# Second input projection: convolutions accumulated in PSUM, transposes behind the next product

## The chip, the cores and the metric

The kernel runs on one NeuronCore of a Trainium2 chip. The metric is the device time of one execution in microseconds. The engines are called as in the profile: PE is TensorE (PEld its weight loads), DVE VectorE, ACT ScalarE, POOL GpSimd, SP the queue that issues most DMAs. PSUM has eight banks of 512 fp32 columns on 128 partitions; a tile of 128x1024 fp32 takes two of them.

## The reference

Two transformer-like blocks over 1024 tokens of width 1024 in fp32. The first (gated recurrence and attention, then a mixture of 16 experts) isn't touched. Of the second, the change touches what follows:

```python
h = layer_norm(x, ln_emb_g, ln_emb_b)
proj = jnp.einsum('bld,de->ble', h, w_in[i])
xs, z, bm, cm, dt_raw, glu, cgate = jnp.split(proj, SPLITS_2, axis=-1)
xbc = jax.nn.silu(causal_depthwise_conv(concatenate([xs, bm, cm]), ssm_conv_w, ssm_conv_b))   # 4 taps
dt = jax.nn.softplus(dt_raw + dt_bias);  a = -jnp.exp(a_log)
y = ssd_chunked(xh, dt, a, bm_c, cm_c) + d_skip * xh      # 8 chunks of 128 tokens, decays exp(cumsum)
yz = y * silu(z)                                          # then a normalisation in 2 groups
u = (glu[..., :1024] + b) * sigmoid(glu[..., 1024:] + b)
u = causal_depthwise_conv(u, conf_conv_w, conf_conv_b)    # 31 taps
u = silu(layer_norm(u)) * silu(cgate)
```

## The kernel before

Products are taken in three matmuls each (`mm3`, L136): every fp32 operand is split into a high part, a cast by ACT, and a low part, a subtraction by DVE or POOL (`split`, L127). A product of a 128-channel tile with 1024 tokens is 48 matmuls of 512 columns into a two-bank PSUM tile "big", of which there are three (pool `pq`, L1213); one more two-bank tile "tr" (pool `pt1`, L1214) takes transposes.

`in_proj2` (L1198) normalises the input in two halves (`turned`, L1219: transposes, the high part by ACT, a full-precision copy `hf` in SBUF, the low part by DVE or POOL), then calls, in an order written out at L1426 to L1442, for j = 0 to 7 `glu(j)`, and between them `bc` (B and C), `dts` (step sizes) and `xs` (four calls), and then the gate products `z`.

`glu(j)` makes two products and `u`, and `conv_tail` (L1270) its 31-tap convolution: tap 0 and taps 1 to 5 as scaled passes by ACT, added up on POOL into `acc` in SBUF, and taps 6 to 30 as `scalar_tensor_tensor` on DVE. The DVE taps go into a list `bgq` with a cost each, from which `bg(us)` (L1092) emits as many as its budget allows, after each product. `last` stores `acc` and adds it to `s1` on POOL.

`xbc` (L1324) copies a product into SBUF (`xl`, ACT), convolves it with four DVE instructions, applies Silu on ACT, and, for B and xs, transposes the result on PE straight away into "tr"; `bc` and `xs` copy that out. `dts` does the same for the step sizes, then a `log1p` chain of small DVE instructions and two matmuls of prefix sums. `s1`, when all eight convolutions are added, is summed over channels on PE (`chan_sum`, L1449) in the middle of `z(2)`, and `mu` in SBUF is subtracted in `centred`.

The state-space part (`decays` L1605, `chunk` L1633, `ssd` L1695) makes for each chunk the decay matrix `M`: DVE and POOL scale triangles, PE sums them into a one-bank tile "seg" (two of them), ACT writes the exponential into SBUF, and DVE multiplies it by `cbm`. `chunk` uses the PSUM tiles "po" (twice) and "pyd".

The program is written with a framework that orders each engine's instructions when it is built, by an estimate of its own of when each can start (L1897), and puts in the semaphores; on the chip each engine runs its list in that fixed order and waits where an operand or a buffer isn't ready. So instructions that stand together in the code, as the four of a convolution, may stand apart with taps between them.

Of the kernel before, what the change touches and what calls it, by code (L numbers as in the profile page):

```python
# [18 lines left out]
P = 128  # L19
S = 1024  # L20
# [17 lines left out]
NPT = 6  # L38
# [74 lines left out]
class Core:  # L113
# [1084 lines left out]
    def in_proj2(self, cl):  # L1198
# [20 lines left out]
        def turned(half, xts):  # L1219

            hs = slice(half * 512, half * 512 + 512)
            for k2 in range(KT // 2):
                pt = pq.tile([P, 2, 512], F, name="big") if half == 0 and k2 % 3 else pt1.tile([P, 2, 512], F, name="tr")
                hf = st.tile([P, S + 4], F, name="xl")[:, 0:D].rearrange("p (a b) -> p a b", a=2)
                for q in range(2):
# [44 lines left out]
        def conv_tail(j, u):  # L1270
            acc = cf.tile([P, S], F, name="acc", bufs=3)
            w = lambda t: self.col("conf_conv_w", j * 31 + t)
            nc.scalar.activation(acc, u[:, 0:S], AF.Identity, bias=self.col("conf_conv_b", j), scale=w(0))
            for t in range(1, NPT):
                tmp = cf.tile([P, S], F, name="tmp")
                nc.scalar.activation(tmp, u[:, t:t + S], AF.Copy, scale=w(t))  # L1276
                nc.gpsimd.tensor_add(acc, acc, tmp)  # L1277

            def tap(t):
                nc.vector.scalar_tensor_tensor(acc, u[:, t:t + S], w(t), acc, op0=ALU.mult, op1=ALU.add)  # L1280

            def last():
                nc.sync.dma_start(self.ucd[j * P:(j + 1) * P, :], acc)
                if j == 0:
                    nc.gpsimd.tensor_copy(s1, acc)
                else:
                    nc.gpsimd.tensor_add(s1, s1, acc)
# [8 lines left out]
        def glu(j):  # L1296
# [25 lines left out]
            self.bg(17.0)  # L1322

        def xbc(j, ps, dst):  # L1324

            xl = st.tile([P, S + 4], F, name="xl")
            nc.vector.memset(xl[:, 0:3], 0.0)
            nc.scalar.copy(xl[:, 3:S + 3], ps)
            a = ct(0)
            w = lambda t: self.col("ssm_conv_w", j * 4 + t)  # L1330
            nc.vector.tensor_scalar(a, xl[:, 0:S], w(0), self.col("ssm_conv_b", j), op0=ALU.mult, op1=ALU.add)
            for t in range(1, 4):
                nc.vector.scalar_tensor_tensor(a, xl[:, t:t + S], w(t), a, op0=ALU.mult, op1=ALU.add)
            nc.scalar.activation(dst, a, AF.Silu)
            pt = pt1.tile([P, NB, P], F, name="tr")
            if j < 10:
                for b in range(NB):
                    nc.tensor.transpose(pt[:, b], dst[:, b * P:(b + 1) * P], self.ident)
            return pt

        def bc(which):
            w = weights(W[:, 2048 + which * 256:2304 + which * 256])
            dst = (self.BT, self.CT)[which]
            for g in range(2):
                pt = xbc(8 + which * 2 + g, proj(w, g), dst[:, g])
                if which == 0:
                    nc.scalar.copy(self.Bk[:, :, g * P:(g + 1) * P], pt)
                self.bg(5.0)

        def xs(jj):  # L1350
            w = weights(W[:, jj * 256:(jj + 1) * 256])
            for i in range(2):
                j = jj * 2 + i
                t = ct(1)
                pt = xbc(j, proj(w, i), t)
                o = st.tile([P, NB, P], F, name="t2", bufs=1)
                nc.scalar.copy(o, pt)
                nc.sync.dma_start(self.xsd[:, j * P:(j + 1) * P].rearrange("(b p) c -> p b c", p=P), o)
                self.bg(5.0)

        def dts():
# [3 lines left out]
            raw = st.tile([NE, S], F, name="t2", bufs=1)  # L1365
# [4 lines left out]
            cut = Cut(ct(1))  # L1370
# [11 lines left out]
            adt = cut.tile([P, P], F, "adt").rearrange("p (b h) -> p b h", b=NB)  # L1382
            nc.vector.scalar_tensor_tensor(adt, self.dt, -1.0, al[:, None, :].to_broadcast([P, NB, NE]), op0=ALU.mult,
                                           op1=ALU.mult)
            self.split(self.adtH, self.adtL, adt)
            self.adtH, self.adtL = self.adtH.bitcast(F), self.adtL.bitcast(F)
            pt = pt1.tile([P, NB, P], F, name="tr")
            nc.tensor.matmul(pt[:, 0], self.U, f(adt), start=True, stop=True)
            nc.tensor.matmul(pt[:, 1], self.ones, f(adt), start=True, stop=True)
            tot = cut.tile([P, P], F, "tot")  # L1390
            nc.scalar.copy(tot, pt[:, 1])
            nc.vector.tensor_sub(e, tot, pt[:, 0])
            nc.scalar.activation(e, e, AF.Exp)
            nc.vector.tensor_mul(f(self.ddt), f(self.dt), e)
            nc.scalar.activation(f(self.cdec), tot, AF.Exp)
            nc.scalar.activation(f(self.eacs), pt[:, 0], AF.Exp)
# [52 lines left out]
        def chan_sum(s):  # L1449
            ps = pq.tile([P, S], F, name="big")  # L1450
# [450 lines left out]
```

## Time and profile before

| | us |
|---|---|
| median of 3 runs (lowest, highest) | 2415.98 (2408.94, 2416.17) |
| the profiled execution | 2410.97 |
| its span, first to last instruction | 2409.0 |
| PE busy | 2103.6 |
| DVE busy | 2006.4 |
| ACT busy | 1151.8 |
| POOL busy | 742.4 |
| mean granted clock of TensorE | 0.932 |

The span is the time from the first to the last instruction of the profiled execution. A group's line gives the total busy time, the mean of one instruction and the idle time of the engine just before them, with what ended it. The list of waits says who waited for whom. The granted clock is 1.0 where the engine runs at 2.4 GHz and 0.5 where it runs at 1.2; a mean between them is a mix of the two.

### The profile page before, as it was taken

Reading aid. Unit: us, or ns where it says so; the run is one execution under the profiler, and the core shown is the slowest. Engines: PE = TensorE matmul, PEld = TensorE weight load, DVE = VectorE, ACT = ScalarE, POOL = GpSimd, SP = SyncE. Lnnn points to the kernel's source line nnn. Section 1 sums busy time; section 2 is a strip of 40 time slices with the busy share of each in tenths; the row PEclk is TensorE's granted clock in tenths of the full one; section 3 lists DMA queues with packets and bytes.
Section 4 is the critical chain, followed back from the end, with each engine's and each line's share of the span. In section 5 each row is a group of like instructions: output and inputs, shape, how many; then the busy total and the mean of one; then the engine's idle time right before and its main releaser. Section 6 shows DMA issues by size and latency. Waiting matters only on the chain. (4 is left out here: it accounts for less than half of the span.)

```text
span 2409.0 us, 26895 instructions
## 1 busy us (share of the span) xinstructions
PE 2103.6 (87%) x10158; PEld 1725.8 (72%) x10158; DVE 2006.4 (83%) x2389; ACT 1151.8 (48%) x1365; POOL 742.4 (31%) x320
## 2 busy tenths in 40 slices
PE   4899899979899999988996978677796988788997
PEld 3678679868778888777884766556595876567785
DVE  8687869977878998878897399999998779995776
ACT  4484749842257777656775433232222443334111
POOL 2333300030202122112211455444552266563000
PEclk8899999989889999999997989888898998889999
DMA  7433373137489999988984111122224453336212
GB/s 251 149 126 116 117 175 99 65 95 283 151 335 369 386 379 393 358 295 309 393 307 132 45 27 53 35 70 61 61 71 150 156 202 122 122 114 244 76 56 70
DMA packets 213857, 422.88 MB, mean 176 GB/s; under 512 B 46144, under 2 KB 118080, under 8 KB 213600
## 3 DMA queue, kind: packets, MB, share of 16 engines
q1 hardware_dynamic: 198528, 380.27, 45.5%
q0 software_dynamic: 9440, 34.61, 4.7%
q10 hardware_dynamic: 5760, 6.29, 0.7%
q8 instruction: 80, 1.31, 0.2%
q14 instruction: 49, 0.40, 0.0%
HBM read 362.35 MB, written 58.77 MB: 175 GB/s over the span
## 5 line engine op out<-in xcount | busy, mean ns | idle before, releaser
L130 ACT CAST wH<-wr 128x2048 fp32r<-128x2048 f32 (+1 forms) x262 | 437.8, 1678 | 206.4 <-PE big L143 156.3
L134 DVE TENSOR_TENSOR wL<-wr,wH 128x2048 fp32r<-128x2048 f32 (+1 forms) x197 | 463.2, 2369 | 82.6 <-ACT wH L130 81.2
L1280 DVE SCALAR_TENSOR_TENSOR acc<-u,cols,acc 128x1024 f32<-128x1024 f32 x200 | 364.9, 1856 | 1.9
L141 PE MATMUL big<-hL,wH 128*128 128x512 f32 (+1 forms) x720 | 289.3, 403 | 6.3 <-DVE hL L326 6.2
L140 PE MATMUL big<-hH,wH 128*128 128x512 f32 (+1 forms) x720 | 284.1, 400 | 9.4 <-ACT B L410 3.7
L134 POOL TENSOR_TENSOR wL<-wr,wH 128x1024 fp32r<-128x1024 f32 (+2 forms) x66 | 188.8, 2871 | 251.2 <-ACT wH L130 236.1
L143 PE MATMUL big<-hH,wL 128*128 128x512 f32 (+1 forms) x720 | 232.4, 401 | 0.0
L140 PEld LDWEIGHTS big<-hH,wH 128*128 128x128 f32 (+1 forms) x720 | 137.5, 191 | 43.5 <-ACT hH L324 4.4
L141 PEld LDWEIGHTS big<-hL,wH 128*128 128x128 f32 (+1 forms) x720 | 138.5, 192 | 39.5 <-DVE hL L326 6.5
L143 PEld LDWEIGHTS big<-hH,wL 128*128 128x128 f32 (+1 forms) x720 | 138.0, 192 | 31.5 <-issue 0.9
L140 PE MATMUL big<-hH,aH 128*128 128x512 f32 x384 | 154.3, 403 | 6.3 <-ACT aH L130 2.8
L140 PE MATMUL big<-wH,0H 128*128 128x512 f32 x384 | 152.6, 397 | 3.6 <-ACT 0H L130 3.6
L141 PE MATMUL big<-wL,1H 128*128 128x512 f32 x384 | 153.7, 400 | 2.3 <-DVE wL L134 2.3
L141 PE MATMUL big<-wL,0H 128*128 128x512 f32 x384 | 154.1, 401 | 0.0
L141 PE MATMUL big<-hL,aH 128*128 128x512 f32 x384 | 152.9, 399 | 0.9 <-DVE hL L1526 0.9
L140 PE MATMUL big<-wH,1H 128*128 128x512 f32 x384 | 151.5, 395 | 2.0 <-ACT 1H L130 2.0
L140 PE MATMUL big<-wH,hH 128*128 128x256 f32 (+1 forms) x448 | 151.3, 338 | 1.9 <-ACT B L410 1.7
L141 PE MATMUL big<-wL,hH 128*128 128x256 f32 (+1 forms) x448 | 149.1, 333 | 0.0
L143 PE MATMUL big<-wH,hL 128*128 128x256 f32 (+1 forms) x448 | 148.8, 332 | 0.0
L1005 POOL DMA_INDIRECT xe<-h2d,idx x16 | 43.4, 2710 | 339.9 <-issue 252.3
L1277 POOL TENSOR_TENSOR acc<-acc,tmp 128x1024 f32<-128x1024 f32 x40 | 124.5, 3114 | 34.5 <-ACT tmp L1276 18.5
L143 PE MATMUL big<-wH,1L 128*128 128x512 f32 x384 | 120.4, 395 | 7.6 <-DVE 1L L134 7.6
(539 smaller groups left out, 4842.0 us busy)
## 6 DMA issues: line engine op xcount, KB each, us to landing
wr<-in_w_dram SPq DMA_DIRECT2D x192, 1024.0 KB, 8.3
wr<-in_w_in_dram SPq DMA_DIRECT2D x48, 512.0 KB, 6.5
wm<-in_w_mod_dram SPq DMA_DIRECT2D x32, 512.0 KB, 4.0
wm<-in_w_mod_dram SPq DMA_DIRECT2D x8, 1024.0 KB
wr<-in_w_in_dram SPq DMA_DIRECT2D x32, 256.0 KB, 3.1
u<-ucd SPq DMA_DIRECT2D x16, 512.0 KB, 3.4
wr<-in_w_out_dram SPq DMA_DIRECT2D x14, 512.0 KB, 6.1
xt<-in_x_dram SPq DMA_DIRECT2D x12, 512.0 KB, 9.1
```

The costliest lines, as they stand in the source:

```text
L130: self.high = nc.scalar.copy(h, src)
L134: (le or nc.vector).tensor_sub(l, src, h)
L140: mm(o, aH, bH, start=start, stop=False)
L141: mm(o, aH, bL, start=False, stop=False)
L143: mm(o, aL, bH, start=False, stop=stop)
L1005: nc.gpsimd.indirect_dma_start(out=xe, out_offset=None, in_=self.h2d, in_offset=bass.IndirectOffsetOnAxis(ap=idx[:, :1], axis=0))
L1277: nc.gpsimd.tensor_add(acc, acc, tmp)
L1280: nc.vector.scalar_tensor_tensor(acc, u[:, t:t + S], w(t), acc, op0=ALU.mult, op1=ALU.add)
```

## The change

`conv_tail` accumulates in the PSUM tile "tr": ACT writes tap 10 with the bias (`begin`), DVE adds taps 11 to 30 there, ACT and POOL make a side sum `part` of taps 0 to 9 in SBUF, its steps put between the taps, and DVE joins both in `last`. `xbc` reads the product from PSUM. The transposes, the step sizes (`steps`) and the prefix sums (`sums`) go into a list `later` that `proj` runs after its own matmuls, into "big" tiles. `turned` keeps the scaled copy in PSUM. `mu` lies in "tr". In the state space, the exponential stays in "seg", and the tiles "po"/"pyd" become "y" (for the outputs of both kinds) and "s" (for the states). `bg` budgets and costs change. "..." marks what is left out.

```diff
-NPT = 6
+NPT = 10
...
-                hf = st.tile([P, S + 4], F, name="xl")[:, 0:D].rearrange("p (a b) -> p a b", a=2)
...
                     if half:
-                        nc.vector.tensor_scalar(hf[:, q], pt[:, q], g, b, op0=ALU.mult, op1=ALU.add)
+                        nc.vector.tensor_scalar(pt[:, q], pt[:, q], g, b, op0=ALU.mult, op1=ALU.add)
                     else:
-                        self.evac = nc.scalar.activation(hf[:, q], pt[:, q], AF.Identity, bias=b, scale=g)
-                    (nc.gpsimd if q else nc.vector).tensor_sub(hL[k][:, hs], hf[:, q], hH[k][:, hs])
+                        self.evac = nc.scalar.activation(pt[:, q], pt[:, q], AF.Identity, bias=b, scale=g)
+                    nc.vector.tensor_sub(hL[k][:, hs], pt[:, q], hH[k][:, hs])
...
+        later = []
+
+        def after():
+            fns = later[:]
+            later.clear()
+            for fn in fns:
+                fn()
...
                          kt == 0, kt == KT - 1)
+            after()
             return ps
...
         def conv_tail(j, u):
-            acc = cf.tile([P, S], F, name="acc", bufs=3)
+
             w = lambda t: self.col("conf_conv_w", j * 31 + t)
-            nc.scalar.activation(acc, u[:, 0:S], AF.Identity, bias=self.col("conf_conv_b", j), scale=w(0))
-            for t in range(1, NPT):
-                tmp = cf.tile([P, S], F, name="tmp")
-                nc.scalar.activation(tmp, u[:, t:t + S], AF.Copy, scale=w(t))
-                nc.gpsimd.tensor_add(acc, acc, tmp)
+            acc, part = [], []
+
+            def begin():
+                acc.append(pt1.tile([P, S], F, name="tr"))
+                nc.scalar.activation(acc[0], u[:, NPT:NPT + S], AF.Identity, bias=self.col("conf_conv_b", j), scale=w(NPT))
+
+            def side(t):
+                if t == 0:
+                    part.append(cf.tile([P, S], F, name="acc", bufs=3))
+                    nc.scalar.activation(part[0], u[:, 0:S], AF.Copy, scale=w(0))
+                else:
+                    tmp = cf.tile([P, S], F, name="tmp")
+                    nc.scalar.activation(tmp, u[:, t:t + S], AF.Copy, scale=w(t))
+                    nc.gpsimd.tensor_add(part[0], part[0], tmp)
 
             def tap(t):
-                nc.vector.scalar_tensor_tensor(acc, u[:, t:t + S], w(t), acc, op0=ALU.mult, op1=ALU.add)
+                nc.vector.scalar_tensor_tensor(acc[0], u[:, t:t + S], w(t), acc[0], op0=ALU.mult, op1=ALU.add)
 
             def last():
-                nc.sync.dma_start(self.ucd[j * P:(j + 1) * P, :], acc)
+                nc.vector.tensor_add(part[0], acc[0], part[0])
+                nc.sync.dma_start(self.ucd[j * P:(j + 1) * P, :], part[0])
...
-            for t in range(NPT, 31):
-                self.bgq.append((1.13, lambda t=t: tap(t)))
-            self.bgq.append((0.0, last))
+            side(0)
+            self.bgq.append((0.0, begin))
+            for i, t in enumerate(range(NPT + 1, 31)):
+                if i % 2 == 0 and i // 2 + 1 < NPT:
+                    self.bgq.append((0.0, lambda t=i // 2 + 1: side(t)))
+                self.bgq.append((1.22, lambda t=t: tap(t)))
+            self.bgq.append((1.22, last))
...
-            self.bg(17.0)
+            self.bg(15.0)
 
         def xbc(j, ps, dst):
 
-            xl = st.tile([P, S + 4], F, name="xl")
-            nc.vector.memset(xl[:, 0:3], 0.0)
-            nc.scalar.copy(xl[:, 3:S + 3], ps)
             a = ct(0)
             w = lambda t: self.col("ssm_conv_w", j * 4 + t)
-            nc.vector.tensor_scalar(a, xl[:, 0:S], w(0), self.col("ssm_conv_b", j), op0=ALU.mult, op1=ALU.add)
-            for t in range(1, 4):
-                nc.vector.scalar_tensor_tensor(a, xl[:, t:t + S], w(t), a, op0=ALU.mult, op1=ALU.add)
+            nc.scalar.activation(a, ps, AF.Identity, bias=self.col("ssm_conv_b", j), scale=w(3))
+            for k in range(1, 4):
+                nc.vector.scalar_tensor_tensor(a[:, k:S], ps[:, 0:S - k], w(3 - k), a[:, k:S], op0=ALU.mult, op1=ALU.add)
             nc.scalar.activation(dst, a, AF.Silu)
-            pt = pt1.tile([P, NB, P], F, name="tr")
-            if j < 10:
-                for b in range(NB):
-                    nc.tensor.transpose(pt[:, b], dst[:, b * P:(b + 1) * P], self.ident)
-            return pt
+
+        def turn(src, fn):
+
+            pt = pq.tile([P, NB, P], F, name="big")
+            for b in range(NB):
+                nc.tensor.transpose(pt[:, b], src[:, b * P:(b + 1) * P], self.ident)
+            fn(pt)
...
-                pt = xbc(8 + which * 2 + g, proj(w, g), dst[:, g])
+                xbc(8 + which * 2 + g, proj(w, g), dst[:, g])
                 if which == 0:
-                    nc.scalar.copy(self.Bk[:, :, g * P:(g + 1) * P], pt)
-                self.bg(5.0)
+                    later.append(lambda g=g: turn(dst[:, g], lambda pt: nc.scalar.copy(self.Bk[:, :, g * P:(g + 1) * P], pt)))
+                self.bg(7.0)
...
-                pt = xbc(j, proj(w, i), t)
-                o = st.tile([P, NB, P], F, name="t2", bufs=1)
-                nc.scalar.copy(o, pt)
-                nc.sync.dma_start(self.xsd[:, j * P:(j + 1) * P].rearrange("(b p) c -> p b c", p=P), o)
-                self.bg(5.0)
+                xbc(j, proj(w, i), t)
+                later.append(lambda j=j, t=t: turn(t, lambda pt: store(j, pt)))
+                self.bg(7.0)
...
-            pt = pt1.tile([P, NB, P], F, name="tr")
+            later.append(lambda: steps(raw))
+
+        def steps(raw):
+
+            pt = pq.tile([P, NB, P], F, name="big")
...
+            def sums():
+                pt = pq.tile([P, NB, P], F, name="big")
+                nc.tensor.matmul(pt[:, 0], self.U, adt, start=True, stop=True)
...
+            later.append(sums)
...
-        mu = cp.tile([P, S], F, name="mu")
-        z(2, mid={ZM: [lambda: nc.scalar.activation(mu, chan_sum(s1), AF.Copy, scale=1.0 / D)]})
+        mu = pt1.tile([P, S], F, name="tr")
+        z(2, mid={ZM: [lambda: nc.scalar.activation(mu, chan_sum(s1, mu), AF.Copy, scale=1.0 / D)]})
...
-                    M = Mg[:, q * 4:q * 4 + 4]
-                    nc.scalar.activation(M.rearrange("p h l -> p (h l)"), sg, AF.Exp)
-                    nc.vector.tensor_mul(M, M, cbm[:, None, :].to_broadcast([P, 4, P]))
+                    nc.scalar.activation(sg, sg, AF.Exp)
+                    nc.vector.tensor_mul(Mg[:, q * 4:q * 4 + 4], sg.rearrange("p (h l) -> p h l", l=P),
+                                         cbm[:, None, :].to_broadcast([P, 4, P]))
...
-                po = psum("po")
+                po = psum("y")
...
-                ps = psum("po")
+                ps = psum("s")
...
-            pyd = psum("pyd")
+            pyd = psum("y")
...
-            nc.vector.tensor_add(xs, pyd, xs)
-            nc.vector.tensor_mul(xs, xs, sz)
+            nc.vector.tensor_add(pyd, pyd, xs)
+            nc.vector.tensor_mul(xs, pyd, sz)
```

## Rows read from the trace of the kernel before

**Rows 1.** The page's slices of the whole span, busy tenths in 40 slices

```profile
DVE  8687869977878998878897399999998779995776
...
PEclk8899999989889999999997989888898998889999
```

**Rows 2.** Table of stretches: us of each engine busy (instructions), clock, DMA

```profile
1372.60:1845.00 472.40, 362.65 (x1823) 304.67 (x1823) 460.57 (x301) 145.84 (x152) 244.14 (x80) 0.88 0.19 57
1845.00:1945.00 100.00, 100.00 (x455) 81.95 (x456) 68.48 (x44) 38.45 (x37) 26.39 (x15) 0.98 0.50 169
1990.00:2150.00 160.00, 132.34 (x567) 102.08 (x566) 154.22 (x168) 57.66 (x147) 99.10 (x48) 0.87 0.33 112
```

**Rows 3.** List of waits, PE alone, 1372.6 to 1866: total us, times, longest

```profile
PE tr L1338 <- ACT t L1334: 47.5, 3, 17.1
PE tr L1388 <- DVE t L1383: 21.1, 1, 21.1
PE big L1452 <- POOL s L1287: 20.1, 1, 20.1
PE tr L1338 <- ACT BT L1334: 12.1, 2, 11.0
PE tr L1369 <- ACT t L1366: 8.7, 1, 8.7
```

**Rows 4.** Table of stretches again, after one wait and in a stretch without

```profile
1480.00:1500.00 20.00, 18.99 (x77) 15.65 (x78) 20.00 (x18) 7.51 (x10) 9.56 (x3) 0.82 0.16 53
1640.00:1660.00 20.00, 20.00 (x89) 16.33 (x87) 19.82 (x12) 8.63 (x8) 16.00 (x6) 1.00 0.18 53
```

**Rows 5.** Groups of instructions, DVE, 1372.6 to 1845: busy us, mean ns, idle before

```profile
L1280 DVE SCALAR_TENSOR_TENSOR acc<-u,cols,acc 128x1024 f32<-128x1024 f32 x200 | 364.9, 1856 | 1.9
L1333 DVE SCALAR_TENSOR_TENSOR t<-xl,cols,t 128x1024 f32<-128x1024 f32 x36 | 56.1, 1557 | 0.1
L1320 DVE SCALAR_TENSOR_TENSOR u<-t,t 128x1024 f32<-128x1024 f32 x8 | 14.5, 1816 | 4.6 <-ACT t L1317 4.1 <-ACT t L1315 0.5
```

**Rows 6.** POOL: one line's shortest/median/longest ns, then a group of 1372.6 to 1845

```profile
L1277 POOL TENSOR_TENSOR acc<-acc,tmp x40: 2393/3260/3566, 1377.8 to 1786.6; 128x1024 f32<-128x1024 f32 x40
...
L134 POOL TENSOR_TENSOR wL<-wr,wH 128x1024 fp32r<-128x1024 f32 x30 | 93.1, 3109 | 91.4 <-ACT wH L130 88.2 <-PE big L141 3.2
```

**Rows 7.** Timelines of DVE and POOL, 1396 to 1440: start us, us, instruction, count

```profile
1399.45 13.32 DVE L1280 SCALAR_TENSOR_TENSOR acc<-u,cols,acc 128x1024 f32<-128x1024 f32 x4
1415.44 1.27 DVE L1280 SCALAR_TENSOR_TENSOR acc<-u,cols,acc 128x1024 f32<-128x1024 f32 x1
1416.63 1.27 DVE L1333 SCALAR_TENSOR_TENSOR t<-xl,cols,t 128x1024 f32<-128x1024 f32 x1
1423.92 13.37 DVE L1280 SCALAR_TENSOR_TENSOR acc<-u,cols,acc 128x1024 f32<-128x1024 f32 x11
...
1404.97 6.71 POOL L1277 TENSOR_TENSOR acc<-acc,tmp 128x1024 f32<-128x1024 f32 x2
```

**Rows 8.** DVE, single lines: shortest/median/longest ns, first and last start us

```profile
L1662 DVE TENSOR_TENSOR xs<-pyd,xs x7: 1209/1216/1225, 2013.7 to 2178.8; 128x1024 f32<-128x1024 f32 x7
...
L1663 DVE TENSOR_TENSOR xs<-xs,sz x8: 1210/1222/3410, 1992.5 to 2180.1; 128x1024 f32<-128x1024 f32 x8
...
L1076 DVE SCALAR_TENSOR_TENSOR y<-big,g,gate x1: 1284/1284/1284, 1294.0 to 1294.0; 128x1024 f32<-128x1024 f32 x1
```

**Rows 9.** Groups of instructions, ACT, 1372.6 to 1845

```profile
L1276 ACT ACTIVATE tmp<-u,cols 128x1024 f32<-128x1024 f32 x40 | 45.1, 1149 | 40.1 <-POOL acc L1277 40.1
L1334 ACT ACTIVATE t<-t 128x1024 f32<-128x1024 f32 x8 | 8.5, 1061 | 79.7 <-DVE t L1333 77.6 <-DVE ddt L1394 2.1
```

**Rows 10.** DVE groups, 1990 to 2150; shortest/median/longest ns of one line

```profile
L1629 DVE TENSOR_TENSOR M<-M,cbm 128x512 f32<-128x512 f32 x22 | 27.5, 1252 | 1.3 <-ACT M L1628 1.3
L1663 DVE TENSOR_TENSOR xs<-xs,sz 128x1024 f32<-128x1024 f32 x6 | 8.8, 1466 | 0.0
...
L1629 DVE TENSOR_TENSOR M<-M,cbm x32: 675/688/2882, 1955.5 to 2173.9; 128x512 f32<-128x512 f32 x32
```

More of the change, by code (lines that the diff above doesn't have):

```diff
@@ L1279, in tap @@
             def tap(t):
-                nc.vector.scalar_tensor_tensor(acc, u[:, t:t + S], w(t), acc, op0=ALU.mult, op1=ALU.add)
+                nc.vector.scalar_tensor_tensor(acc[0], u[:, t:t + S], w(t), acc[0], op0=ALU.mult, op1=ALU.add)
             def last():
-                nc.sync.dma_start(self.ucd[j * P:(j + 1) * P, :], acc)
+                nc.vector.tensor_add(part[0], acc[0], part[0])
+                nc.sync.dma_start(self.ucd[j * P:(j + 1) * P, :], part[0])
                 if j == 0:
-                    nc.gpsimd.tensor_copy(s1, acc)
+                    nc.gpsimd.tensor_copy(s1, part[0])
@@ L1286, in last @@
                 else:
-                    nc.gpsimd.tensor_add(s1, s1, acc)
-            for t in range(NPT, 31):
-                self.bgq.append((1.13, lambda t=t: tap(t)))
-            self.bgq.append((0.0, last))
+                    nc.gpsimd.tensor_add(s1, s1, part[0])
+            side(0)
[4 more added lines that the diff above has]
+                self.bgq.append((1.22, lambda t=t: tap(t)))
@@ L1344, in bc, with store @@
             for g in range(2):
-                pt = xbc(8 + which * 2 + g, proj(w, g), dst[:, g])
+                xbc(8 + which * 2 + g, proj(w, g), dst[:, g])
                 if which == 0:
-                    nc.scalar.copy(self.Bk[:, :, g * P:(g + 1) * P], pt)
-                self.bg(5.0)
+                    later.append(lambda g=g: turn(dst[:, g], lambda pt: nc.scalar.copy(self.Bk[:, :, g * P:(g + 1) * P], pt)))
+                self.bg(7.0)
         def xs(jj):
             w = weights(W[:, jj * 256:(jj + 1) * 256])
+            def store(j, pt):
+                o = st.tile([P, NB, P], F, name="t2")
+                nc.scalar.copy(o, pt)
+                nc.sync.dma_start(self.xsd[:, j * P:(j + 1) * P].rearrange("(b p) c -> p b c", p=P), o)
             for i in range(2):
@@ L1364, in dts @@
             ps = proj(weights(W[:, 2560:2576]), 0, NE)
-            raw = st.tile([NE, S], F, name="t2", bufs=1)
+            raw = st.tile([NE, S], F, name="t2")
             nc.scalar.activation(raw, ps[0:NE, :], AF.Identity, bias=self.col("dt_bias")[0:NE])
-            pt = pt1.tile([P, NB, P], F, name="tr")
+            later.append(lambda: steps(raw))
+        def steps(raw):
+            pt = pq.tile([P, NB, P], F, name="big")
             for b in range(NB):
                 nc.tensor.transpose(pt[:, 0, b * NE:(b + 1) * NE], raw[:, b * P:(b + 1) * P], self.ident[0:NE, 0:NE])
-            cut = Cut(ct(1))
+            cut = Cut(sm.tile([P, S], F, name="cut"))
             v = cut.tile([P, P], F, "v")
@@ L1381, in dts @@
             nc.scalar.activation(al, al, AF.Exp)
[L1382 to L1385, printed above, removed]
+            adt = cut.tile([P, P], F, "adt")
+            nc.vector.scalar_tensor_tensor(adt.rearrange("p (b h) -> p b h", b=NB), self.dt, -1.0,
+                                           al[:, None, :].to_broadcast([P, NB, NE]), op0=ALU.mult, op1=ALU.mult)
+            self.split(self.adtH, self.adtL, adt.rearrange("p (b h) -> p b h", b=NB))
             self.adtH, self.adtL = self.adtH.bitcast(F), self.adtL.bitcast(F)
[L1387 to L1396, printed above, removed]
+            def sums():
+                pt = pq.tile([P, NB, P], F, name="big")
+                nc.tensor.matmul(pt[:, 0], self.U, adt, start=True, stop=True)
+                nc.tensor.matmul(pt[:, 1], self.ones, adt, start=True, stop=True)
+                tot = cut.tile([P, P], F, "tot")
+                nc.scalar.copy(tot, pt[:, 1])
+                nc.vector.tensor_sub(e, tot, pt[:, 0])
+                nc.scalar.activation(e, e, AF.Exp)
+                nc.vector.tensor_mul(f(self.ddt), f(self.dt), e)
+                nc.scalar.activation(f(self.cdec), tot, AF.Exp)
+                nc.scalar.activation(f(self.eacs), pt[:, 0], AF.Exp)
+            later.append(sums)
         def z_weights(q):
@@ L1447, in in_proj2, with chan_sum @@
         cp = pool(name="cp", bufs=1)
-        def chan_sum(s):
-            ps = pq.tile([P, S], F, name="big")
+        def chan_sum(s, ps):
             for h in range(2):
@@ L1472, in deviation @@
         def deviation():
-            nc.vector.tensor_scalar(s2, chan_sum(s2), 1.0 / D, LN_EPS, op0=ALU.mult, op1=ALU.add)
+            nc.vector.tensor_scalar(s2, chan_sum(s2, pq.tile([P, S], F, name="big")), 1.0 / D, LN_EPS, op0=ALU.mult, op1=ALU.add)
             nc.scalar.activation(r, s2, AF.Sqrt)
@@ L1698, in ssd @@
         pool = lambda **k: es.enter_context(Even(tc, reuse_waits="tile", **k))
-        pp = {n: pool(name="p" + n, bufs=1, space=PSUM) for n in ("pyd", "po")}
+        pp = {n: pool(name="p" + n, bufs=1, space=PSUM) for n in ("y", "s")}
         psum = lambda n: pp[n].tile([P, D], F, name=n)
```

## The prediction

> **What bounds the kernel now.** I read the page's slices first: DVE is at 9 tenths or more from slice 24 to slice 30, the only such run on an engine other than PE, and PEclk dips in the same slices [rows 1]. The table by stage turns that into the second input projection, 1372.6 to 1845 us of the span: DVE 460.6 of 472.4 us busy, PE 362.7 at a mean granted clock of 0.88. The stage after it keeps PE busy for 100 of 100 us, and the state-space stage has DVE at 154 of 160 us [rows 2]. The list of PE's waits, read next, gives its idle time to five kinds: transposes L1338 that wait for ACT's Silu (47.5 us in 3 waits, 12.1 in 2), the sums L1388 that wait for DVE (21.1), the channel sum L1452 that waits for POOL's s1 (20.1), and the step transposes L1369 (8.7). Together 109.5 us in 8 waits, 7 of them long [rows 3]. All stand behind DVE: Silu waits for the four-tap convolution, s1 for the last tap. So DVE's queue sets this stage, and PE shows it as waits.
>
> Why DVE is late stands in its groups: a tap takes 1856 ns in the mean over 200 taps, a convolution step 1557 [rows 5], but the timeline has the same tap at two rates. 4 taps took 13.32 us (3.3 each) while POOL ran adds back to back at 3.35 each, and later 11 taps took 13.37 (1.215 each) with POOL idle [rows 7]. Two engines taking turns give 3.3 for a pair: both operands of these DVE instructions lie in SBUF, as POOL's do. Where one DVE operand lies in PSUM the spread is gone: `xs<-pyd,xs` has 1209/1216/1225 as its shortest, median and longest, while `xs<-xs,sz`, the next instruction on the same data, reaches 3410, in a stage where POOL works more than half the time [rows 2, 8].
>
> **The change, part by part.** The sum stands against the profiled execution, 2411.0 us (span 2409.0 and 2.0 around it); the median of the three runs is 2416.0, 5 us more.
>
> *Taps.* Of each channel tile's 31 taps, 25 were on DVE and 6 on ACT with 5 adds on POOL; now one tap is written by ACT into PSUM (`begin`), 20 are on DVE with the accumulator in PSUM, 10 on ACT into a side sum in SBUF with 9 POOL adds, and DVE joins the two (`last`). DVE: 200 taps at 1.856 become 160 taps and 8 adds. No row shows a DVE instruction that writes PSUM. Below, the bound is the chained SBUF rate 1.215; above, 1.856 if the lock stays, and 2.5 if reading and writing one bank in the same instruction takes two passes of 1.27. I take 1.28, because the nearest row, a `scalar_tensor_tensor` with a PSUM operand, a column scalar and an SBUF operand, has 1284 [rows 8]; 160 x 1.28 = 205, and 8 x 1.22 = 10.
>
> *Four-tap convolutions.* ACT now scales the PSUM product straight into `a` (about 1.15, as a scaled ACT pass [rows 9]) in place of a copy; DVE's `tensor_scalar` goes and three steps per tile stay, 36 x 1.28 = 46. With the GLU product (8, 14.5 us as now [rows 5]) and, my estimate, 15 us of small step-size work, DVE needs 205 + 10 + 46 + 14.5 + 15 = 291 us, against 460.6.
>
> *POOL and ACT.* POOL has 72 adds in place of 40, 30 weight splits and 8 for s1: 110 instructions. At the shortest add, 2.39, that is 263 us; at the median with the lock, 3.26, it is 359 [rows 6]. I take 2.4, since few DVE instructions with two SBUF operands are left. ACT: 88 passes x 1.15 in place of 48, +46 on the 145.8 busy now [rows 2, 9]: 192.
>
> *PE.* The count of its instructions is the same. Its 362.7 us hold work at the half level: after the wait that ended at 1481, the stretch 1480 to 1500 has a mean of 0.82, so some 7 us at 1.2 GHz, of which 1 was idle, while 1640 to 1660, without a wait, has 1.00 and 89 matmuls in 20 us (0.225 each, 10.8 for a product of 48) [rows 4]. At 5 us per long wait, 7 waits, half of it lost: 17 us (0 to 21). So with no wait PE needs 362.7 - 17 = 346, more than DVE's 291, POOL's 263 and ACT's 192. **PE becomes the bound of the stage.**
>
> *Moved transposes.* `turn`, `steps` and `sums` now run behind the following product. From the end of a product to the end of Silu: 1.15, three steps each alternating with a tap as they do now at 1.2 [rows 7], 6 x 1.2 = 7.2, and 1.06 of Silu [rows 9], 9.4 with little for semaphores; the product in front lasts 10.8. So a cover of about 1 us, and where DVE has a tap more ahead PE waits that much. `sums` stands behind some 14 chained small DVE steps, each of which may let a tap pass: 14 x 1.5 = 21 against 10.8. I charge 10 turns and `steps` with 1.4 us each and `sums` with 10: 25 us of waits left (0 to 70).
>
> *What is queued behind the new waits.* `begin` waits on ACT for the only "tr" buffer, until `last` of the tile before; behind it in ACT's queue stand the evacuations of the next products, and "big" has three buffers, now also used by the transposes and held through three DVE steps. `last` waits on DVE for POOL's ninth add. In one period (two GLU and two xs products, about 46 us of PE) DVE has some 35 us and POOL 14 x 2.4 = 34, so each has 11 us to catch up; I price these at nothing within the 25. The store of `ucd` on SP's queue waits for `last` instead of the last tap, with the z stores behind it; it comes earlier than now.
>
> *First normalisation, mu.* The scaled copy stays in PSUM and the subtraction leaves POOL: its 8 subtractions of 512 columns go to DVE, just ahead of the first taps. `mu` in PSUM makes 16 subtractions safe from the lock, beside a PE that is busy for the whole stretch [rows 2]. Nothing, as long as PE is the bound there; -2 to +5.
>
> *State space.* The exponential stays in PSUM and DVE multiplies from there: 22 products of 1252 ns in the stretch 1990 to 2150 fall to the line's median, 0.69, 12.4 us, and `xs<-xs,sz`, 6 of 1466, to 1.22, 1.5 us [rows 10]. DVE binds that stretch, but the next instruction with two SBUF operands may inherit the wait for the same POOL instruction; half counted, -7. Against it each of the two "seg" buffers is now held until DVE's multiply, 0.69 us longer or more, and PE may wait for one: -14 to +6. The y/s pools exchange one wait for another; nothing.
>
> Sum: waits -110, clock -17, waits left +25, state space -7: -109, **2302 us**.
>
> One rule of the Trainium skill bears on what no row shows. By its page "SBUF — State Buffer", Who interferes with whom, a DVE instruction contends with GpSimd through its second SBUF input, so an instruction with one SBUF input, wherever it writes, should not; by it the lock goes, by the trace that is shown for PSUM inputs only.
>
> **The rivals.**
>
> *Slower: the PSUM tap takes two passes.* In-place work on one bank at 2.5 us: DVE 160 x 2.5 + 10 + 46 + 14.5 + 15 = 486, with its 12 us of idle 498, +26 on the stage, -7 later: 2430. It decides from a tap of (460.6 - 86)/160 = 2.34. For it: no row has such an output. Against: reading PSUM costs nothing extra in any row [rows 8]. Chance 0.07.
>
> *The lock stays, or POOL binds.* If DVE and POOL still take turns, DVE needs 160 x 1.856 + 10 + 36 x 1.557 + 14.5 + 15 = 392 and POOL 359, chained by `last`; stage some 405, -67, state space 0: 2344 (2330 to 2365). For it: four more taps per tile go to the engine that needs 2.4 to 3.3 where DVE needs 1.28. Against: the 1209/1216/1225 row. Chance 0.13. The Trainium skill, "GPSIMD Engine Reference", 4.1 Engine selection, speaks against the move too: elementwise work belongs on VectorE. By that rule this rival's sum would hold; by the rows, only if the lock does.
>
> *The waits return at the hand-over.* The queues are in an order fixed beforehand, and turns with 1 us of cover may each cost 5 us, `sums` 15: 70 us left in place of 25, 2347 (2335 to 2380). For it: alternation and the three "big" buffers; against: 11 us of slack a period. Chance 0.12.
>
> *Nothing moves*: the gains and new waits cancel, 2404 to 2418. Chance 0.03.
>
> **How the numbers follow.** Forecast 0.65, 2266 (no waits left, clock 21, state space -14) to 2330. The range reaches to the two middle rivals: 2265 to 2370, leaving out the slow case, the unmoved one and the tails. Within 0.3% (7 us) is about what a measurement of this kernel can't tell from no change. Faster 0.65 + 0.13 + 0.12 = 0.90, same 0.03, slower 0.07.
>
> **What would show it.** Right: tap groups near 1.28 with no instance above 1.4; POOL adds near 2.4; DVE near 80% busy in the stage; PE's waits in the stage under 40 us and PEclk near 1.0; stage near 365 us instead of 472. Wrong: taps over 1.8; ACT waiting long for `begin` or PE for "big"; PE waits at `turn` of 5 us each.

## The result and the profile after

The changed kernel takes 2308.83 us in the median of 4 runs (2305.33 to 2310.75), the kernel before 2415.28 on the same chip: ratio 0.9563, 95% interval 0.9543 to 0.9583. The forecast was 2302, with a range of 2265 to 2370. The profiled execution took 2310.75 us (span 2308.9), 100.2 less than that of before (2410.97).

Where those 100 us went, from the start of one landmark to the start of the next in the two traces (each landmark is one instruction: the first transpose of the normalised input, the first product `u`, the channel sum of `s1`, the first and the last output matmul of the chunks, the first addition of `finish`):

| stretch | before, us | after, us | difference |
|---|---|---|---|
| up to the first transpose | 1313.7 | 1314.7 | +1.0 |
| first normalisation, up to the first `u` | 58.9 | 63.3 | +4.4 |
| second input projection, up to the channel sum | 472.4 | 373.8 | -98.6 |
| up to the first chunk's output | 125.8 | 124.0 | -1.8 |
| state space | 207.7 | 198.3 | -9.4 |
| up to `finish` | 38.0 | 35.8 | -2.2 |
| `finish` to the end | 192.5 | 199.0 | +6.5 |

The page's slices of after, busy tenths in 40 slices, answer to [rows 1]:

```profile
DVE  8677859977878988987788739968864678986676
...
PEclk8899999998979999999999799899999988999998
```

The run of nines on DVE from slice 24 to 30 is gone, and PEclk is at 9 in those slices but for one 8 (a slice is 57.7 us here and 60.2 in [rows 1]). The table of stretches (us of PE, PEld, DVE, ACT and POOL busy, with their counts of instructions, then the granted clock, DMA share and GB/s) shows the projection, the stretch behind it, and the middle of the state space, as [rows 2] do for before:

```profile
1378.01:1751.80 373.79, 349.74 (x1821) 295.68 (x1821) 289.58 (x247) 189.75 (x189) 260.98 (x112) 0.97 0.25 77
1751.80:1852.00 100.20, 100.20 (x475) 83.24 (x474) 64.29 (x47) 39.49 (x38) 25.38 (x17) 1.00 0.44 152
1895.00:2055.00 160.00, 139.10 (x608) 107.46 (x607) 146.38 (x169) 55.31 (x140) 101.21 (x51) 0.91 0.37 125
```

In the projection PE is now the busiest engine, 349.7 of 373.8 us at a mean clock of 0.97, and DVE is at 289.6. The list of PE's waits in that stretch (total us, times, longest) has three entries where [rows 3] had five long kinds:

```profile
PE big L1420 <- DVE cut L1413: 22.1, 1, 22.1
PE big L1360 <- ACT t L1354: 1.9, 1, 1.9
PE big L140 <- ACT t L1340: 0.7, 1, 0.7
```

L1420 is the first matmul of the prefix sums (`sums`), L1360 the transposes of `turn`. DVE's and POOL's groups of the same stretch (busy us, mean ns, idle before), against [rows 5] and [rows 6]:

```profile
L1298 DVE SCALAR_TENSOR_TENSOR tr<-u,cols,tr 128x1024 f32<-128x1024 f32 x160 | 205.7, 1285 | 17.7 <-ACT tr L1286 14.2
L1343 DVE SCALAR_TENSOR_TENSOR u<-t,t 128x1024 f32<-128x1024 f32 x8 | 19.6, 2450 | 38.6 <-ACT t L1338 33.7 <-ACT t L1340 4.9
L1353 DVE SCALAR_TENSOR_TENSOR t<-big,cols,t 128x1023 f32<-128x1023 f32 x12 | 15.4, 1279 | 1.0 <-ACT t L1351 1.0
L1301 DVE TENSOR_TENSOR acc<-tr,acc 128x1024 f32<-128x1024 f32 x8 | 9.8, 1223 | 2.4 <-POOL acc L1295 1.8
...
L1295 POOL TENSOR_TENSOR acc<-acc,tmp 128x1024 f32<-128x1024 f32 x72 | 173.1, 2406 | 33.3 <-ACT tmp L1294 29.5 <-ACT cut L1402 0.4
L134 POOL TENSOR_TENSOR wL<-wr,wH 128x1024 fp32r<-128x1024 f32 x30 | 72.2, 2409 | 65.9 <-ACT wH L130 65.9
```

And single lines of after with their shortest, median and longest ns:

```profile
L1298 DVE SCALAR_TENSOR_TENSOR tr<-u,cols,tr x160: 1201/1290/1291, 1383.7 to 1720.3; 128x1024 f32<-128x1024 f32 x160
...
L1661 DVE TENSOR_TENSOR M<-seg,cbm x32: 673/678/692, 1860.3 to 2072.4; 128x512 f32<-128x512 f32 x32
...
L1654 DVE TENSOR_TENSOR VH<-iota,adtH x32: 676/1755/3054, 1850.8 to 2062.4; 128x512 fp32r<-128x512 f32 x32
```

Every one of the 160 taps lies between 1201 and 1291 ns, beside a POOL that is 261 us busy. What still has both operands in SBUF has the old spread, from what the prediction calls the lock, DVE and POOL taking turns: `u<-t,t` went from 1816 to 2450 in the mean, and `VH` of the state space has a median of 1755 and a longest of 3054.

### The profile page after: what moved, and what is told of

Same layout as the page of the kernel before. It is cut to its first block, busy times and chain, and to the rows that moved or that the text cites. A ratio compares the mean times of both kernels' runs of the same rounds, so it can differ in the third digit from the quotient of the medians.

```text
span 2308.9 us, 26964 instructions
## 1 busy us (share of the span) xinstructions
PE 2089.4 (90%) x10158; PEld 1717.0 (74%) x10158; DVE 1810.7 (78%) x2341; ACT 1197.2 (52%) x1403; POOL 743.5 (32%) x344
## 5 line engine op out<-in xcount | busy, mean ns | idle before, releaser
L134 POOL TENSOR_TENSOR wL<-wr,wH 128x1024 fp32r<-128x1024 f32 (+2 forms) x66 | 164.3, 2497 | 272.8 <-ACT wH L130 252.4
L1298 DVE SCALAR_TENSOR_TENSOR tr<-u,cols,tr 128x1024 f32<-128x1024 f32 x160 | 205.7, 1285 | 17.7 <-ACT tr L1286 14.2
L1295 POOL TENSOR_TENSOR acc<-acc,tmp 128x1024 f32<-128x1024 f32 x72 | 173.1, 2406 | 33.3 <-ACT tmp L1294 29.5
```

Of the source, the lines that this page charges most:

```text
L134: (le or nc.vector).tensor_sub(l, src, h)
L1295: nc.gpsimd.tensor_add(part[0], part[0], tmp)
L1298: nc.vector.scalar_tensor_tensor(acc[0], u[:, t:t + S], w(t), acc[0], op0=ALU.mult, op1=ALU.add)
```

## The experiments

Times are medians; a ratio is against runs of the kernel before in the same session, with its 95% interval, and so stands beside 0.9563 of the changed kernel. "The stage" is the second input projection, the third row of the table above. "..." stands for lines that are left out.

**The accumulator back in SBUF.** The changed kernel in all but the place of the taps' sum and, to make room for it, one buffer instead of two for the tile "t2" (as in the kernel before).

```diff
-                acc.append(pt1.tile([P, S], F, name="tr"))
+                acc.append(cf.tile([P, S], F, name="accs", bufs=1))
...
-                o = st.tile([P, NB, P], F, name="t2")
+                o = st.tile([P, NB, P], F, name="t2", bufs=1)
...
```

> The changed kernel with the tap accumulator in SBUF instead of PSUM, nothing else of the convolution moved (one buffer of the step-size and store tile is given up for the space). If the place of the accumulator carries the gain, taps go back from 1.285 us to 1.8 or more, POOL adds from 2.4 to 3.2, DVE has some 276 us of unhindered work plus 110 POOL instructions that each hold it up by about 1.75 (the 40% of 80 seen before), 468 us: stage 465 to 500, total 2400 to 2440. If the smaller number of taps on DVE carries it, the stage stays near 374 us and the total near 2309 to 2325.

Measured: 2428.75 us, ratio 1.0057 (1.0036 to 1.0078). The whole gain is lost, and a little more. DVE's taps, POOL's adds, and two of PE's waits:

```profile
L1298 DVE SCALAR_TENSOR_TENSOR accs<-u,cols,accs 128x1024 f32<-128x1024 f32 x160 | 351.6, 2197 | 16.4 <-ACT accs L1286 12.8
...
L1295 POOL TENSOR_TENSOR acc<-acc,tmp 128x1024 f32<-128x1024 f32 x72 | 228.5, 3175 | 45.2 <-ACT tmp L1294 41.7
...
PE big L1360 <- ACT t L1354: 49.3, 7, 12.5
PE big L1420 <- DVE cut L1413: 45.2, 1, 45.2
```

The same 160 instructions take 2197 ns in place of 1285 and POOL's 72 adds 3175 in place of 2406; PE waits 120 us again and the stage lasts 489.5. The single "t2" is not what costs this: ACT stood idle 2 us in all before the copies into it. Without the accumulator in PSUM nothing of the gain is left, though the four-tap convolutions still read from PSUM here. Whether the accumulator would do without them was not run.

**The moved transposes alone**, in the kernel before: those of B and xs go behind the next product, still into "tr". The step sizes and the prefix sums stay where they were.

```diff
...
+            after()
             return ps
...
-                pt = xbc(j, proj(w, i), t)
...
+                xbc(j, proj(w, i), t)
+                later.append(lambda j=j, t=t: turn(t, lambda pt: store(j, pt)))
```

> The kernel before with one part of the change: the transposes of B and xs go behind the next product (the step sizes stay where they were). If the lock between DVE and POOL and DVE's full queue carry the gain, DVE keeps its 460 us of work in a stage of 472, so at most 12 us can come off: 2400 to 2418, and PE's waits move to another place instead of going. If the hand-over carries it, the 47.5 + 12.1 us that PE waited for these transposes go: 2345 to 2360.

Measured: 2414.35 us, ratio 1.0003 (0.9994 to 1.0013). Nothing moves, and PE's waits are those of [rows 3], line by line:

```profile
PE tr L1349 <- ACT t L1343: 47.7, 3, 17.2
PE tr L1403 <- DVE t L1398: 21.2, 1, 21.2
PE big L1467 <- POOL s L1296: 20.8, 1, 20.8
PE tr L1349 <- ACT BT L1343: 12.1, 2, 11.0
PE tr L1384 <- ACT t L1381: 8.9, 1, 8.9
```

PE's list of instructions is nearly the same as before: with a pool of their own the transposes had already been put one to two products later when the program was ordered (40 to 117 matmuls, at 48 to a product, after ACT began to copy theirs), and still came too early for DVE.

**The transposes at once**, in the changed kernel: only `turn` is called directly; `steps` and `sums` stay behind the next product.

```diff
...
-                later.append(lambda j=j, t=t: turn(t, lambda pt: store(j, pt)))
+                turn(t, lambda pt: store(j, pt))
```

> The changed kernel with the transposes of B and xs written right behind their own product again (step sizes and sums still behind the next). If PE needs the written order, each of 10 transposes waits some 9.4 us for the convolution and Silu: +60 to +95, 2370 to 2400. If DVE's queue carries the gain, the framework puts the transposes behind the following product by itself, since their operand is ready only then, and the time stays within 8 us of 2309.

Measured: 2384.36 us, ratio 0.9881 (0.9857 to 0.9904), some 75 us over the changed kernel: the first of the two cases put on record, not the one within 8 us. All of PE's waits in the stage:

```profile
PE big L1360 <- ACT t L1354: 70.2, 8, 9.8
PE big L1360 <- ACT BT L1354: 18.3, 2, 9.9
```

Ten waits of some 9 us, each the time from a product's end to its Silu: here the transposes do stand right behind their own product, with none of another between. The likely reason is that they share the "big" tiles with the products, and that those were handed out in the order of the code; this was not tried by itself. So the two parts belong together: the accumulator takes "tr" away from the transposes, and once they are in "big" the code's order has to give them their distance.

**The prefix sums four products later.**

`after` counts down the products for what lies in `held`.

```diff
...
-            later.append(sums)
+            held.append([4, sums])
```

> The changed kernel with the prefix sums four products later than the change puts them. PE's one long wait of the stage, 22.1 us at L1420, is for the step-size chain, whose small DVE instructions each let a tap pass; behind four more products of 10.8 us it should be gone, with 2 us of half clock after it: 2283 to 2290. If PE would only wait elsewhere for the same DVE work, the time stays at 2300 to 2309.

Measured: 2282.76 us, ratio 0.9459 (0.9440 to 0.9479), 26 us under the changed kernel. PE's waits in the stage:

```profile
PE big L1364 <- ACT t L1358: 7.8, 2, 7.3
PE big L140 <- ACT t L1344: 0.7, 1, 0.7
```

The 22.1 us are gone; the first turn of xs, just behind, which had waited 1.9, now waits 7.3. The stage takes 356.0 us (-17.8), and the state space 192.0 (-6.3), which is taken up below. Why `sums` waited so long is on DVE's timeline of the changed kernel (start us, us, instruction):

```profile
1480.77 1.55 DVE L188 SCALAR_TENSOR_TENSOR cut<-cut 128x128 f32<-128x128 f32 x1
1482.24 1.28 DVE L1298 SCALAR_TENSOR_TENSOR tr<-u,cols,tr 128x1024 f32<-128x1024 f32 x1
1483.44 0.28 DVE L188 SCALAR_TENSOR_TENSOR cut<-cut 128x128 f32<-128x128 f32 x1
1483.64 1.28 DVE L1298 SCALAR_TENSOR_TENSOR tr<-u,cols,tr 128x1024 f32<-128x1024 f32 x1
...
1488.88 2.17 DVE L188 SCALAR_TENSOR_TENSOR cut<-cut 128x128 f32<-128x128 f32 x1
1490.97 1.28 DVE L1298 SCALAR_TENSOR_TENSOR tr<-u,cols,tr 128x1024 f32<-128x1024 f32 x1
1492.16 1.31 DVE L188 SCALAR_TENSOR_TENSOR cut<-cut 128x128 f32<-128x128 f32 x1
```

and on POOL's:

```profile
1488.55 9.64 POOL L1295 TENSOR_TENSOR acc<-acc,tmp 128x1024 f32<-128x1024 f32 x4 [6.37 <-ACT tmp L1294]
```

The small steps of the `log1p` chain alternate with taps, as forecast, and a step of 0.28 us takes up to 2.17 where POOL is at an add: both its operands are in SBUF. From the first step at 1471.8 to `adt` at 1501.1 that makes 29 us, and PE had been at `sums` since 1479.1.

**Six taps instead of ten on ACT and POOL.**

```diff
-NPT = 10
+NPT = 6
...
-            self.bg(15.0)
+            self.bg(18.0)
```

> The changed kernel with the split of the taps as before: 6 on ACT and POOL, 24 on DVE in PSUM and one begun by ACT (the budget after each GLU pair goes from 15 to 18 for the longer list). DVE gets 32 taps of 1.285 more, 41 us, and has 333 us of work in a stage of 374 that PE binds at 346. If the place of the accumulator is what counts, the cover takes nearly all of it: 2309 to 2322. If moving four taps per tile to ACT and POOL was itself needed, the 41 us show: 2340 to 2352.

Measured: 2299.17 us, ratio 0.9518 (0.9504 to 0.9533): 10 us faster than the changed kernel, not slower. DVE is busy 325.8 us of the stage instead of 289.6 and POOL 184.7 instead of 261.0; the stage falls by 5.2 us (the wait for `sums` 19.4 instead of 22.1, and none at the turns), the state space by 5.6. With the lock off the taps, moving four of them per tile to ACT and POOL bought nothing: it cost these 10 us.

**The exponential back in SBUF**, in the changed kernel:

```diff
...
-                    nc.scalar.activation(sg, sg, AF.Exp)
+                    nc.scalar.activation(M.rearrange("p h l -> p (h l)"), sg, AF.Exp)
...
```

> The changed kernel with the exponential of the state space in SBUF again, so DVE's multiply by cbm has two SBUF operands. If the 9.4 us that the state-space stage lost come from this, the mean of that multiply goes from 0.69 to about 1.25 us and the time to 2314 to 2320. If the wait only moves to the next DVE instruction with two SBUF operands, the time stays within 4 us of 2309.

Measured: 2317.98 us, ratio 0.9602 (0.9589 to 0.9616), +9; the state space takes 209.3 us instead of 198.3. In it the masked product `M` goes from 678 ns in the mean to 1315, and `VH` from 1837 to 1397.

**The state-space part alone**, in the kernel before, its edits as in the change:

```diff
...
+                    nc.scalar.activation(sg, sg, AF.Exp)
+                    nc.vector.tensor_mul(Mg[:, q * 4:q * 4 + 4], sg.rearrange("p (h l) -> p h l", l=P),
...
+            nc.vector.tensor_add(pyd, pyd, xs)
+            nc.vector.tensor_mul(xs, pyd, sz)
```

> The kernel before with the state-space part of the change alone (exponential and sums kept in PSUM, the tiles y and s). Theory: this part is a gain of its own, since DVE binds the stretch and its products with two SBUF operands wait for POOL; the stage (first to last output tile of the chunks) falls from 207.7 us to 198 to 201 and the total from 2414 to 2403 to 2408, ratio 0.9955 to 0.9975. Products with the mask near 0.69 us in all cases. Rival: the 9.4 us that the changed kernel gains in this stage come from the queues that it inherits from the projection; then this kernel stays at 2411 to 2417.

Measured: 2397.0 us, ratio 0.9933 (0.9908 to 0.9958): 16 to 18 us, more than expected. The state space takes 191.0 us in place of 207.7. DVE's groups in it, of the kernel before:

```profile
L1629 DVE TENSOR_TENSOR M<-M,cbm 128x512 f32<-128x512 f32 x28 | 38.1, 1360 | 2.1 <-ACT M L1628 2.1
L1621 DVE TENSOR_TENSOR VH<-iota,adtH 128x512 fp32r<-128x512 f32 x25 | 33.7, 1354 | 0.0
```

and of this kernel:

```profile
L1621 DVE TENSOR_TENSOR VH<-iota,adtH 128x512 fp32r<-128x512 f32 x25 | 46.8, 1874 | 0.0
L1628 DVE TENSOR_TENSOR M<-seg,cbm 128x512 f32<-128x512 f32 x28 | 19.0, 679 | 3.3 <-ACT seg L1627 3.3
```

The masked product loses 19.1 us, and `VH`, which keeps both operands in SBUF, gains 13.1: two thirds of what the one lost turn up at the other, and with the exponential back in SBUF (above) the two moved the other way. DVE's busy time there falls from 196.8 to 181.1.

**The first normalisation's copy back in SBUF**, with half of its subtractions on POOL, in the changed kernel:

```diff
+                hf = st.tile([P, S], F, name="t2").rearrange("p (a b) -> p a b", a=2)
...
-                        nc.vector.tensor_scalar(pt[:, q], pt[:, q], g, b, op0=ALU.mult, op1=ALU.add)
+                        nc.vector.tensor_scalar(hf[:, q], pt[:, q], g, b, op0=ALU.mult, op1=ALU.add)
...
-                    nc.vector.tensor_sub(hL[k][:, hs], pt[:, q], hH[k][:, hs])
+                    (nc.gpsimd if q else nc.vector).tensor_sub(hL[k][:, hs], hf[:, q], hH[k][:, hs])
```

> The changed kernel with the scaled copy of the first normalisation in SBUF and half of its subtractions on POOL again, as in the kernel before. The stretch from the first transposes to the first u went from 58.9 to 63.4 us with the change. If holding the PSUM tile until DVE's subtraction does that, 2303 to 2306; if it is another cause (the order of the first products), 2307 to 2311.

Measured: 2295.05 us, ratio 0.9508 (0.9495 to 0.9521), -14. The first stretch is back at 58.9 us. Its PE waits behind the first transposes were, in the changed kernel,

```profile
PE big L140 <- ACT hH L1229: 3.1, 1, 3.1
PE tr L1227 <- DVE hL L1234: 1.6, 1, 1.6
PE big L141 <- DVE hL L1234: 0.8, 1, 0.8
```

and what stands in their place here sums to 0.4. 1.6 us of the 5.5 were a wait for a PSUM tile that DVE's subtraction held and 0.8 for its result; the 3.1 were for ACT's high part, and what made that late is not shown. Nor were the copy and POOL's share of the subtractions set apart. The stretch is 4.5 of the 14 us; the stage brings 1.6, the state space 7.8 and the end 2.4 (the two profiled executions differ by 16.8).

**Both of these together** (late sums, copy in SBUF):

> The prefix sums four products later and the scaled copy of the first normalisation in SBUF, together. The two lie in different stretches of PE's queue, so they should add up: 26 and 4.5 us off 2309, 2277 to 2281. If DVE or POOL were the next bound behind the removed wait, no better than 2283.

Measured: 2280.38 us, ratio 0.9441 (0.9428 to 0.9453), the fastest version: 28 us under the changed kernel where the two alone gave 26 and 14. Their gains in the state space are the same one: 6.3 and 7.8 us alone, 5.8 together.

**All three** (and six taps on ACT and POOL):

> The changed kernel with three edits together: prefix sums four products later, scaled copy of the first normalisation in SBUF with half of its subtractions on POOL, and six taps instead of ten on ACT and POOL. The first two together gave 2280.4. The third alone took 10 us off the changed kernel, 5 of them between the first and the eighth GLU product, 6 in the state space. Theory: the 5 us are a gain of its own and the 6 are the same that the other edits bring: 2273 to 2277. Rival: with the sums' wait gone PE is the bound of the stage and fewer adds on POOL change nothing: 2279 to 2283; or four more taps per tile on DVE bring waits back at the turns: over 2284.

Measured: 2299.4 us, ratio 0.9521 (0.9504 to 0.9539), 19 us slower than without the third. PE's two long waits from the first `u` to beyond the channel sums:

```profile
PE big L1490 <- DVE s L1507: 9.2, 1, 9.2
PE big L1365 <- ACT t L1359: 8.3, 2, 7.9
```

L1490 is the second channel sum, which waits for DVE's centred squares. With the sums' wait gone PE is earlier, and DVE with its four taps more per tile is late at the end of its list. The 20 us for which PE stood at `sums` had been the time in which DVE caught up: from the first `u` to the first chunk's output six taps take 492.6 us with the wait and 492.5 without it, and ten take 480.4 without it. So the ten taps cost 10 us in the kernel as changed, and are worth some 19 once that wait is gone; some 5 of either are the state space, below.

**What is left open: 192 or 198 us in the state space.** The same source takes 198.3 us in the changed kernel, 197.6 with the accumulator in SBUF and 197.3 with all three edits, but 190 to 193 in the others; the three long ones of that source have DVE idle for 5.6 to 5.8 us at the third chunk's load. DVE's timeline of the changed kernel at that load (start us, us, instruction, idle before):

```profile
1915.58 1.22 DVE L1695 TENSOR_TENSOR y<-y,xs 128x1024 f32<-128x1024 f32 x1
1922.40 1.23 DVE L1669 TENSOR_TENSOR xdt<-xs,dt 128x1024 f32<-128x1024 f32 x1 [5.59 <-DMA xs<-xsd]
1923.54 4.70 DVE L1654 TENSOR_TENSOR VH<-iota,adtH 128x512 fp32r<-128x512 f32 x2
```

and that of the kernel with late sums:

```profile
1898.51 1.22 DVE L1699 TENSOR_TENSOR y<-y,xs 128x1024 f32<-128x1024 f32 x1
1899.64 5.38 DVE L1658 TENSOR_TENSOR VH<-iota,adtH 128x512 fp32r<-128x512 f32 x1
1905.43 1.23 DVE L1673 TENSOR_TENSOR xdt<-xs,dt 128x1024 f32<-128x1024 f32 x1 [0.41 <-DMA xs<-xsd]
```

The load is as late in both, but DVE's list has `xdt` ahead of `VH` in one and behind it in the other: an edit hundreds of microseconds earlier changed the order that was fixed when the program was built. I tried to take the wait away with a third buffer for x, so that the load needn't wait for the first chunk's store:

```diff
-            xs = st.tile([P, D], F, name="xs")
+            xs = st.tile([P, D], F, name="xs", bufs=3)
...
-            sz = st.tile([P, D], F, name="sz")
+            sz = st.tile([P, D], F, name="sz", bufs=1)
```

> The changed kernel with three buffers instead of two for the chunks' x rows (and, for the room, one instead of two for the gate rows), so that the third chunk's load doesn't wait for the first chunk's store. In the changed kernel DVE stands 5.6 us idle there, with the product xdt at the head of its list; in the kernels whose state space took 192 us it had 0.4. Theory: those 5.6 us are what the state space is longer by: stage 192 to 194 us instead of 198.3, total 2302 to 2305. Rival: DVE has slack there, or the single buffer of the gate rows brings a wait of its own: 2307 to 2315.

> The same three buffers in the kernel with late prefix sums and the scaled copy in SBUF (2280.4), where DVE has only 0.4 us of idle time at that load. Theory: nothing to win, 2278 to 2283. Rival: later loads too come ahead and the stage shortens further, under 2277; or the gate rows' single buffer costs, over 2284.

Measured: 2312.22 us, ratio 0.9572 (0.9556 to 0.9588), and 2287.43, 0.9476 (0.9461 to 0.9492). The idle time is gone and the state space is longer, 203.9 and 202.2 us. DVE's group `xdt` in it, first of the changed kernel:

```profile
L1669 DVE TENSOR_TENSOR xdt<-xs,dt 128x1024 f32<-128x1024 f32 x7 | 14.6, 2088 | 5.6 <-DMA xs<-xsd 5.6
```

and then of the same with three buffers:

```profile
L1669 DVE TENSOR_TENSOR xdt<-xs,dt 128x1024 f32<-128x1024 f32 x7 | 22.5, 3214 | 0.0
```

With the wait gone `xdt` stands elsewhere among POOL's additions; one of the slow ones, with what POOL does meanwhile (start us, us):

```profile
1978.44 2.35 POOL L1599 TENSOR_TENSOR rs<-rs,lg 128x1024 f32<-128x1024 f32 x1 [4.30 <-DVE rs L1598]
1980.87 2.39 POOL L1600 TENSOR_TENSOR rs<-rs,bo 128x1024 f32<-128x1024 f32 x1
...
1980.91 3.43 DVE L1669 TENSOR_TENSOR xdt<-xs,dt 128x1024 f32<-128x1024 f32 x1
```

`xdt` is not the whole of it either: its 7.9 us are more than made good by `VH`, 45.8 to 31.5, and the single buffer for the gate rows was not tried by itself. So the 5.6 us of idle time go with the state spaces of 197 to 198 us, but that they are the cause is not shown. With one source this part took 190.1 to 198.3 us, and up to 203.9 with the other buffers; the order, and which instructions of DVE and POOL meet, are the likely reason, and neither was set apart from the other.

## Why the prediction was right, point by point

*The bound.* Right: DVE's queue set the stage through the lock. The tap was put at 1.28 us and measured 1.285 with no instance above 1.291; in SBUF it is 2.197. The Trainium skill, "SBUF — State Buffer", Who interferes with whom, states that a DVE instruction with at most one SBUF input, outside the 2-port modes, does not contend with GpSimd. The trace agrees for an instruction that also writes its sum to PSUM, with 1285 against 2197 ns.

*Busy times.* DVE 289.6 (forecast 291), POOL 261.0 (263), ACT 189.8 (192). PE 349.7 against 346: of its busy time 30.5 us lay at the 1.2 GHz level before and 6.7 do after, which gives back half of the difference, 11.9, not 17. That term was mis-sized by about 5 us.

*Queues behind the new waits.* Priced at nothing, and PE's list has no wait for a free "big" tile; DVE's 14.2 us behind `begin` don't show on PE.

*Waits left.* The sum was right by luck, 24.8 us against 25, and its parts were not. Ten turns and `steps` at 1.4 each came to 1.9 in all, and `sums` to 22.1 instead of 10. Turns were given 1 us of cover, but while PE stands at `sums` DVE gets ahead: with that wait gone, one turn waits 7.3. For `sums` I counted the taps between the small steps and not that the steps themselves wait for POOL: the chain took 29 us in place of 21, and PE had 7 us of other work while it ran, not 10.8.

*The moved transposes.* I priced them as a charge on the gain. By themselves those of B and xs are worth nothing (ratio 1.0003), and without them the change loses 75 of its 106 us: the rival that the waits return at the hand-over is what the kernel would have been with the transposes in "big" and no delay, at 2384 even above its range of 2335 to 2380.

*Stage.* -98.6 us against -102; 373.8 against 365 to 371. What is missing is the clock's term.

*State space.* -9.4 against -7, inside -14 to +6. That the two are so near is in part luck: alone the part gave 16 to 18 us, over twice the term, since `xs<-xs,sz` (12.2 to 8.5 us) and small steps lost waits too. The charge for "seg" was not needed: PE's waits there for DVE's multiply are 4.9 us in that run and 9.3 in the changed kernel, where before it waited 9.7 for ACT's exponential. In the changed kernel DVE's busy time falls as far (196.8 to 181.2), but its idle time grows by 6.2.

*First normalisation.* I booked nothing, with +5 as the upper end; it costs 4.4, and with the old form it is gone. The failed step is "as long as PE is the bound there": with the copy in PSUM and all subtractions on DVE PE waits 5.5 us there in place of 0.4, at least 1.6 of them for the tile that is held longer.

*Later stages.* The sum has no term for them and gives no reason, and that was wrong: `finish` to the end is 6.5 us longer. PE's busy time there rises from 171.2 to 177.3, with 11.1 us at the 1.2 GHz level instead of 3.4. The kernel with the state-space part alone has 199.3 in this stretch too, and the one with the moved transposes alone, which is no faster than before, 196.1. What before it sets the clock's level was not tried.

*Rivals.* The two-pass tap is excluded (1.285). The lock didn't stay; with it the kernel would have taken 2429, not 2344: the rival was under-priced, by 55 of these 85 us because the locked taps take 2.20 with nine adds per tile on POOL, and I had carried over 1.856 from five. By the Trainium skill, "GPSIMD Engine Reference", 4.1 Engine selection, elementwise work belongs on VectorE, and I gave that rule weight only if the lock holds. Six taps instead of ten on ACT and POOL took 2299 against 2309, as the rule has it, but with late sums and the copy in SBUF 2299 against 2280, against it: which engine is late at the end of the stage made the difference here.

## What to carry to other kernels

Where DVE and GpSimd both stream from SBUF, put one operand of DVE's long chains into PSUM; count what that PSUM tile was used for, since the work that it displaces (here transposes) needs another buffer and a new place in the order. Then look at what chain of small dependent steps is left and give its consumer several products of distance: here that was worth a quarter as much as the change itself. And after such an edit read the stages behind it again: the order of their instructions is made anew.

## What the runs showed of the hardware that I had not expected

A `scalar_tensor_tensor` of 128x1024 that reads and writes the same PSUM tile costs what one does that reads PSUM and writes SBUF: 1285 ns against 1276 (steps of 1021 to 1023 columns), with a spread of 90 ns over 160 instances.

The time that the lock takes from one instruction goes in part to the next that has both operands in SBUF: 19.1 us less on `M`, 13.1 more on `VH`. (`u<-t,t` rose from 1816 to 2450 ns, but has 2198 with the accumulator in SBUF as well, so the freed taps account for less than half of it at most.) Short instructions are hit hardest in proportion: a 128x128 step of 0.28 us took up to 2.17.
